# Two attentions with V stationary in column halves and the z of the first SSD group as filler, and an expert scatter kept for the last six pairs

## The chip, the cores and the metric

One core of a Trainium2 chip runs the whole program. The metric is the device time of one execution in microseconds (us). Matrix products run on TensorE (PE; its weight loads are PEld), elementwise work on VectorE (DVE), ScalarE (ACT) and GpSimd (POOL), and SyncE (SP), ACT and POOL issue DMAs. Each engine works through its own queue in order.

## The reference, cut to what matters

Two transformer blocks on 512 tokens of width 1024. The first has spatial gating, a sliding-window attention, an attention to 256 memory tokens, and a gate z. The second has a top-k attention, a state-space branch (SSD) in four groups with a gate z, and a mixture of 32 experts (MoE), two for each token.

```python
# block 1, both attentions: four heads of 64
out = einsum('bnhgqj,bnjhd->bnqhgd', softmax(logits), vb)
y = concatenate([y_a, y_b, y_c]) * silu(z);  x = x + rms_norm(y @ w_out)
# block 2, attention: 16 heads of 64, 4 key/value heads, keys <= query block
o = einsum('bqhgk,bqkhd->bqhgd', softmax(logits), v_sel)
# SSD: conv + silu on xs, B, C; chunked scan; then
y_ssd = group_rmsnorm(y * silu(z)) * g
merged = sigmoid(gate_a) * (y_attn @ w_a) + sigmoid(gate_b) * (y_ssd @ w_b)
x = x + merged @ w_out
# MoE: for each expert e
act = silu(h @ w_gate[e]) * (h @ w_up[e]) * combine[:, e]
out += act @ w_down[e]
```

## The kernel before

The program runs as a chain of stages: block 1 with its attentions (110 to 206 us of the profile), block 2's projections and index scores, block 2's attention (393 to 541), the SSD groups one after another (from 541), the branch merge, and the experts (from about 1010 us to the end). Large products with float32 precision are made of three float32r matmuls of 512 columns each (`gemm_t`, L224 to L226), with the weight split in a high and a low part by ACT (L173) and DVE or POOL (L175). Generators are woven by `mix`: a main generator says how many us of filler it needs at each step, and a filler generator of dense gemms is advanced by so much. Outside the experts, the order within an engine is then made by the compiler's scheduler; in the experts the order on PE is the order of the code.

**Attention of block 1.** `pipeline` runs eight units (two kinds, four query blocks) through five stages `logits`, `expo`, `ptrans`, `pvmul`, `otrans`. `pvmul` takes the transposed probabilities pT (128 keys x 128 queries) as the stationary operand and V (128 x 64) as the moving one (L755), multiplies the result by the reciprocal row sums on DVE (L758), and `otrans` transposes it back by two PE transposes (L768) and a DVE copy (L769). The filler is one u gemm and three z gemms.

**Attention of block 2.** The same five stages for 32 units (four kv heads, two pairs of heads, four query blocks): `pvmul` L1085, the DVE product L1088, the transpose L1098 into a PSUM tile that is held for four units, and an ACT copy L1101. Its filler is `gates`, 16 gemms of 24 matmuls each, the first of which are already used up under the index scores.

**SSD.** `ssd_gemm(g)` makes B and C, xs in two gemms, and z in two gemms; `conv_silu` works on each gemm's output on DVE (L1184, L1190, L1196) and ACT; `silu_from` (L450, L455) works on z. `ssd_chain(g)` is mixed with the gemms of group g + 1. For group 0 all five gemms run ahead of its chain.

**Experts.** There are 16 pairs of experts. For a pair, `gate_up` (L1765, 32 matmul instructions in pairs of column halves) and `down` (L1786, 16 instructions) read weight tiles of 512 KB, twelve for a pair, that SP prefetches in the order of `units`; a new fetch is issued when a tile is read (L1884). Results of most pairs go to a DRAM table by `y_store`, whose DMA is issued on ACT (L1800), and come back by eight indirect DMAs on POOL in `y_fetch` (L1808) and DVE additions (L1810), all at pairs 13 and 14. The pairs in `self.direct` (3, 6, 9, 12, 13, 14, 15) are instead scattered to token rows by matmuls with a one-hot matrix: `slots_t` builds it (L1715, L1720), `y_split` splits the result, `scatter` runs two matmuls (L1871) and a DVE addition (L1873) for each of eight output tiles, in one go after the pair's `down`. Pairs 14 and 15 are scattered in `finish` (L1832 to L1847), which also stores the output. The loop at `for p in range(17)` runs `down(p - 1)` after `gate_up(p)`.

Of the kernel before, what the change touches and what calls it, by code (L numbers as in the profile page):

```python
# [43 lines left out]
class Ker:  # L44
# [412 lines left out]

    def pipeline(self, units, stages, need):
# [65 lines left out]
    def block1(self):  # L524
# [218 lines left out]
        def pvmul(u):  # L743
            kind, n = u
            wk, r, pT = st[u][1], *st[u][4:6]
            po = self.paux()
            nj = wk // P
            for h in range(4):
                for j in range(nj):
                    if kind == 0:  # L750
                        kt = n + 1 - nj + j
                        v = sv[:, kt * P + (h // 2) * 64:kt * P + (h // 2) * 64 + 64]
                    else:
                        v = mv[:, j * 256 + h * 64:j * 256 + h * 64 + 64]
                    nc.tensor.matmul(po[:, h * 64:h * 64 + 64], pT[j][:, h * P:(h + 1) * P], v,  # L755
                                     start=(j == 0), stop=(j == nj - 1))
            o = self.ms([P, 256], "ot")
            nc.vector.tensor_tensor(o.rearrange("p (h d) -> p h d", h=4),  # L758
                                    po[:, :256].rearrange("p (h d) -> p h d", h=4),
                                    r.unsqueeze(2).to_broadcast([P, 4, 64]), op=ALU.mult)  # L760
            st[u] = o

        def otrans(u):
            kind, n = u
            o = st.pop(u)
            po = self.paux()
            for c in range(2):
                nc.tensor.transpose(po[:, c * P:(c + 1) * P], o[:, c * P:(c + 1) * P], self.ident)  # L768
            nc.vector.tensor_copy(c2(oc if kind else ob)[:, :, n * P:(n + 1) * P],  # L769
                                  po[:, :256].rearrange("p (c t) -> p c t", c=2))  # L770
# [21 lines left out]
        mix(self.pipeline(units, (logits, expo, ptrans, pvmul, otrans), 4.5), f2)  # L792
# [77 lines left out]
    def block2(self, hh, hl, ssq):  # L870
# [33 lines left out]
        self.gd = tc.dram_tile([16, P, T], F32, name="scr_g")  # L904

        def gate(i):

            def f(ps):
                t_ = self.t2()
                nc.vector.tensor_tensor(t_, ps[0], rbh, op=ALU.mult)  # L910
                nc.scalar.activation(t_, t_, AF.Tanh)
# [140 lines left out]
        def expo(u):  # L1052
# [6 lines left out]
            r = self.sm([P, 2], "xr")  # L1059
            nc.vector.reciprocal(r, s)  # L1060
            st[u].append(r)
# [17 lines left out]
        def pvmul(u):  # L1079
            kv, c, b = u  # L1080
            po = self.paux()
            r, pts = st[u][2:4]
            for j in range(2):
                for t, pT, i in pts:
                    nc.tensor.matmul(po[:, j * 64:j * 64 + 64], pT[:, i * 256 + j * P:i * 256 + (j + 1) * P],  # L1085
                                     v4[:, t, kv * 64:kv * 64 + 64], start=(t == 0), stop=(t == b))
            o = self.ms([P, P], "ot")
            nc.vector.tensor_tensor(o.rearrange("p (h d) -> p h d", h=2),  # L1088
                                    po[:, :P].rearrange("p (h d) -> p h d", h=2),
                                    r.unsqueeze(2).to_broadcast([P, 2, 64]), op=ALU.mult)  # L1090
            st[u] = o

        def otrans(u):
# [4 lines left out]
            nc.tensor.transpose(po[:, b * P:(b + 1) * P], st.pop(u), self.ident)  # L1098
            if b == NT - 1:
                o = self.t2()  # L1100
                nc.scalar.copy(o, po)  # L1101
# [10 lines left out]
        def attn():  # L1112
            for i, _ in enumerate(self.pipeline(units, (logits, expo, ptrans, pvmul, otrans), 0)):
# [84 lines left out]
    def ssd_gemm(self, g, hh, hl, rb, rbh):  # L1198

        nc = self.nc  # L1200
        u2 = lambda i: [("w2", 2 * (8 + 5 * g + i)), ("w2", 2 * (8 + 5 * g + i) + 1)]
# [21 lines left out]
        return ([self.gemm_t(u2(0), hh, hl, KK, bc_done)] + [self.gemm_t(u2(1 + i), hh, hl, KK, xs_done(i)) for i in range(2)]  # L1223
# [568 lines left out]
    def y_store(self, p, py):  # L1792
# [7 lines left out]
        nc.scalar.dma_start(self.y1d[n:n + P], y)  # L1800

    def y_fetch(self, t):

        nc = self.nc
        x = self.acc[:, t]
        for j in range(2):
            y = self.yf[t % 2 * 2 + j]
            nc.gpsimd.indirect_dma_start(out=y, out_offset=None, in_=self.y1d, in_offset=bass.IndirectOffsetOnAxis(  # L1808
                ap=self.row1[:, t, j:j + 1], axis=0), bounds_check=18 * 64 - 1, oob_is_err=False)
            nc.vector.scalar_tensor_tensor(x, y, self.has1[:, t, j:j + 1], x, op0=ALU.mult, op1=ALU.add)  # L1810
# [12 lines left out]
    def finish(self):  # L1823
# [15 lines left out]
        def late(q, t):  # L1839
# [7 lines left out]
            nc.sync.dma_start(self.out[t][:, s], a)  # L1847
# [39 lines left out]
    def moe_start(self):  # L1887

        self.units = []
        for p in range(17):  # L1890
            self.units += [(e, j) for j in range(4) for e in (2 * p, 2 * p + 1) if p < 16]
            self.units += [(e, j) for j in (4, 5) for e in (2 * p - 2, 2 * p - 1) if p]
# [46 lines left out]
    def moe_body(self, oh, xe):  # L1939
# [5 lines left out]
        at, py = {}, {}  # L1945
# [322 lines left out]
```

## Time and profile before

| | us |
|---|---|
| median of 3 runs (lowest to highest) | 1304.72 (1301.74 to 1309.18) |
| the profiled execution | 1306.37 |
| its span in the trace | 1304.7 |

| engine | busy us of the span |
|---|---|
| PE | 1245.5 |
| PEld | 975.2 |
| DVE | 882.0 |
| ACT | 509.1 |
| POOL | 429.5 |

HBM traffic is 206.0 MB read and 16.1 MB written. Busy time of PE is a union of overlapping, pipelined matmuls, so that what a matmul costs is read from the distance of starts. Ln is line n of the kernel's file.

### The profile page before, as it was taken

The page shows a single profiled execution, that of the slowest core. Times are in us where ns is not written, and L with a number is a line of the kernel's source. Part 1 is how long each engine was busy: PE and PEld are TensorE (multiplying, and loading weights), DVE is VectorE, ACT ScalarE, POOL GpSimd, SP SyncE. Part 2 cuts the span into 40 slices and gives each one's busy share as a digit, 9 for nine tenths or more (in the row PEclk, how much of TensorE's full clock was granted, in tenths as well). Part 3 has the DMA queues.
Part 4 walks back from the last instruction along what each step waited for, and adds up shares of the span by engine and source line. Part 5 has one row for each costly group of instructions (what it writes and reads, how often), then busy time and mean ns, then how long its engine had stood idle before and what let it go on. Part 6 is the DMA issues. An engine that isn't in the chain of part 4 may idle for free. (4 is left out here: it accounts for less than half of the span.)

```text
span 1304.7 us, 18947 instructions
## 1 busy us (share of the span) xinstructions
PE 1245.5 (95%) x7045; PEld 975.2 (75%) x7045; DVE 882.0 (68%) x1700; ACT 509.1 (39%) x942; POOL 429.5 (33%) x474
## 2 busy tenths in 40 slices
PE   6899999999999999999999999999999999999787
PEld 5879888999987888888787887877889744544333
DVE  6598756658998676777988887888683532332255
ACT  6435553355543555443454442443333211111011
POOL 0373323169335431123463343436325110001020
PEclk8899999999999999999999999999999999999889
DMA  7234242052233221134334234385330999999992
GB/s 290 65 92 152 65 144 83 35 160 82 72 106 110 94 98 65 41 116 125 109 96 132 88 105 130 100 288 174 129 135 11 386 374 403 416 414 416 362 412 109
DMA packets 86911, 221.35 MB, mean 170 GB/s; under 512 B 8267, under 2 KB 31467, under 8 KB 86816
## 3 DMA queue, kind: packets, MB, share of 16 engines
q1 hardware_dynamic: 79808, 203.08, 44.6%
q10 hardware_dynamic: 4560, 10.26, 2.1%
q0 software_dynamic: 2448, 6.77, 1.4%
q8 instruction: 56, 0.92, 0.3%
q14 instruction: 39, 0.32, 0.1%
HBM read 205.97 MB, written 16.06 MB: 170 GB/s over the span
## 5 line engine op out<-in xcount | busy, mean ns | idle before, releaser
L175 POOL TENSOR_TENSOR wlo<-tb,whi 128x1024 fp32r<-128x1024 f32 x75 | 191.9, 2559 | 267.7 <-ACT whi L173 267.5
L224 PE MATMUL pmm<-tb,whi 128*128 128x512 f32 x600 | 238.7, 398 | 0.0
L226 PE MATMUL pmm<-tb,wlo 128*128 128x512 f32 x600 | 237.2, 396 | 0.0
L225 PE MATMUL pmm<-tb,whi 128*128 128x512 f32 x600 | 237.0, 395 | 0.0
L173 ACT CAST whi<-tb 128x1024 fp32r<-128x1024 f32 x139 | 144.8, 1044 | 138.6 <-PE pmm L225 57.0
L225 PEld LDWEIGHTS pmm<-tb,whi 128*128 128x128 f32 x600 | 114.0, 190 | 23.6 <-issue 0.9
L226 PEld LDWEIGHTS pmm<-tb,wlo 128*128 128x128 f32 x600 | 113.7, 189 | 24.0 <-issue 0.5
L224 PEld LDWEIGHTS pmm<-tb,whi 128*128 128x128 f32 x600 | 113.8, 190 | 23.2 <-issue 1.2
L175 DVE TENSOR_TENSOR wlo<-tb,whi 128x1024 fp32r<-128x1024 f32 x64 | 82.1, 1284 | 23.2 <-ACT whi L173 23.0
L225 PE MATMUL pmm<-t,whi 128*128 128x512 f32 (+1 forms) x208 | 79.4, 385 | 0.7 <-DVE t L356 0.7
L226 PE MATMUL pmm<-t,wlo 128*128 128x512 f32 (+1 forms) x208 | 79.4, 385 | 0.0
L224 PE MATMUL pmm<-t,whi 128*128 128x512 f32 (+1 forms) x208 | 79.4, 389 | 0.0
L1765 PE MATMUL pmm<-wr,xe 128*64 128x512 f32 x240 | 66.4, 596 | 0.0
L1772 DVE SCALAR_TENSOR_TENSOR th<-th,pmm 128x256 f32<-128x256 f32 x16 | 6.7, 420 | 86.0 <-ACT th L1771 86.0
L1771 ACT ACTIVATE th<-pmm,wcol 128x256 f32<-128x256 f32 x16 | 7.6, 474 | 136.9 <-PE pmm L1765 99.9
L1269 DVE TENSOR_SCALAR t<-t,acs 128x128 f32<-128x128 f32 x128 | 43.8, 408 | 24.2 <-DMA t<-scr_a 24.2
L1190 DVE SCALAR_TENSOR_TENSOR t<-cv,cwh,t 128x512 f32<-128x512 f32 x72 | 56.6, 840 | 0.3 <-ACT t L1187 0.3
L334 PE MATMUL pmm<-whi,tb 128*128 128x256 f32 x192 | 54.8, 285 | 0.0
L336 PE MATMUL pmm<-whi,tb 128*128 128x256 f32 x192 | 54.6, 284 | 0.0
L335 PE MATMUL pmm<-wlo,tb 128*128 128x256 f32 x192 | 54.4, 283 | 0.0
L1057 ACT ACTIVATE tL<-tL,xm 128x128 f32<-128x128 f32 (+3 forms) x64 | 35.4, 554 | 30.6 <-DVE xm L1049 30.4
L225 PEld LDWEIGHTS pmm<-t,whi 128*128 128x128 f32 x208 | 39.2, 188 | 8.4 <-DVE t L356 1.1
(452 smaller groups left out, 2960.3 us busy)
## 6 DMA issues: line engine op xcount, KB each, us to landing
wr<-in_we_dram SPq DMA_DIRECT2D x89, 512.0 KB, 10.1
tb<-in_w_dram SPq DMA_DIRECT2D x78, 512.0 KB, 3.6
tb<-in_we_dram SPq DMA_DIRECT2D x53, 512.0 KB, 10.1
rx<-in_we_dram SPq DMA_DIRECT2D x50, 512.0 KB, 9.0
tb<-in_wo_dram SPq DMA_DIRECT2D x16, 512.0 KB, 3.7
tb<-in_wg_dram SPq DMA_DIRECT2D x16, 512.0 KB, 3.6
t<-scr_a SPq DMA_DIRECT2D x16, 512.0 KB, 5.8
tb<-in_wsb_dram SPq DMA_DIRECT2D x16, 512.0 KB, 3.7
```

The source lines that it names most:

```text
L173: nc.vector.tensor_copy(hi, raw) if dve_hi else nc.scalar.copy(hi, raw)
L175: f = lambda: (nc.gpsimd if pool_lo else nc.vector).tensor_tensor(lo, raw, hi, op=ALU.subtract)
L224: nc.tensor.matmul(ps[c][:, :n], hi[:, s], xh[k], start=first, stop=False)
L225: nc.tensor.matmul(ps[c][:, :n], hi[:, s], xl[k], start=False, stop=False)
L226: nc.tensor.matmul(ps[c][:, :n], lo[:, s], xh[k], start=False, stop=last)
L334: nc.tensor.matmul(o, xh[k][:, ts], hi[:, s], start=(k == 0 and t % 2 == 0), stop=False, **kw)
L335: nc.tensor.matmul(o, xh[k][:, ts], lo[:, s], start=False, stop=False, **kw)
L336: nc.tensor.matmul(o, xl[k][:, ts], hi[:, s], start=False, stop=(k == 7), **kw)
L1057: nc.scalar.activation(L3[:, j], L3[:, j], AF.Exp, bias=m[:, j:j + 1], scale=0.125, accum_out=s[:, j:j + 1])
L1190: nc.vector.scalar_tensor_tensor(y, x[:, i:T + i], w(ct, i), y, op0=ALU.mult, op1=ALU.add)
L1269: nc.vector.tensor_scalar(h8(ab)[:, h], h8(ab)[:, h], self.acs[:, c, 8 * g + h:8 * g + h + 1], 0.0, op0=ALU.subtract, op1=ALU.min)
L1765: nc.tensor.matmul(pg[h * 64:h * 64 + 64], xe[d][:, e + h], w[:, j * 512:(j + 1) * 512], start=(d == 0), stop=(d == 7))
```

## The change

**Attention.** In both `pvmul`, V (64 columns) becomes the stationary operand and pT the moving one (128 columns), two heads side by side in the column halves of PE, so that the result is already transposed. `otrans` is dropped and the pipeline has four stages. The reciprocal sums are spread over the rows by a new helper `rcp_t` (two matmuls with the identity for each two heads), copied by ACT, and applied by one DVE product: in block 1 for each unit, in block 2 once for four units.

**z of group 0.** The four 128-row parts of the first SSD group's z become gates 16 to 19: they are computed as filler of block 2's attention, stored to DRAM without the tanh, and loaded by SP in `ssd_gemm(0)` (`z_load`), which applies the tanh on ACT and the product on DVE. The host packs the weights to match.

**Experts.** `direct` becomes 10 to 15; pairs 0 to 9 go through the table, whose store is issued on POOL. The scatter of pair p - 2 is spread in steps of two tiles between the four `gate_up` steps of pair p. `y_fetch` is split in halves at pairs 11 and 12, and the additions (`y_add`) follow at pair 12 and, spread, in pair 14. `down(14)` moves ahead of `gate_up(15)`, in the fetch order too. The one-hot matrices are built when a scatter pair comes up (14 and 15 together). Output stores alternate between SP and ACT.

```diff
+    def rcp_t(self, out, r):
+        for j in range(2):
+            self.nc.tensor.matmul(out[j * 64:j * 64 + 64], r[:, j:j + 1].to_broadcast([P, 64]), self.ident, ...)
 # block 1 pvmul
-                    nc.tensor.matmul(po[:, h * 64:h * 64 + 64], pT[j][:, h * P:(h + 1) * P], v, ...)
+                        nc.tensor.matmul(po[i * 64:i * 64 + 64, c * P:(c + 1) * P], v, pT[j][:, h * P:(h + 1) * P], ...)
+            for c in range(2):
+                self.rcp_t(pr[:, c * P:(c + 1) * P], r[:, 2 * c:2 * c + 2])
+            nc.scalar.copy(rt, pr[:, :256])
+            nc.vector.tensor_tensor(c2(oc if kind else ob)[:, :, n * P:(n + 1) * P], po..., rt..., op=ALU.mult)
-        mix(self.pipeline(units, (logits, expo, ptrans, pvmul, otrans), 4.5), f2)
+        mix(self.pipeline(units, (logits, expo, ptrans, pvmul), 4.5), f2)
 # block 2
-        gates = chain(*[gate(i) for i in range(16)])
+        gates = chain(*[gate(i) for i in range(20)])
+            for t, pT, i in st.pop(u)[2]:
+                for j in range(2):
+                    nc.tensor.matmul(po[j * 64:j * 64 + 64, b * P:(b + 1) * P], v4[:, t, kv * 64:kv * 64 + 64],
+                                     pT[:, i * 256 + j * P:i * 256 + (j + 1) * P], ...)
             if b == NT - 1:
+                for t in range(NT):
+                    self.rcp_t(pr[:, t * P:(t + 1) * P], r[:, t])
+                nc.scalar.copy(rt, pr)
+                nc.vector.tensor_tensor(o, po, rt, op=ALU.mult)
 # ssd_gemm
+        if g == 0:
+            return first + [z_load()]
 # experts
-        self.direct = [3, 6, 9, 12, 13, 14, 15]
+        self.direct = [10, 11, 12, 13, 14, 15]
-        nc.scalar.dma_start(self.y1d[n:n + P], y)
+        nc.gpsimd.dma_start(self.y1d[n:n + P], y)
+            self.units += gu(p) + (dn(p - 1) if 0 < p < 15 else []) + (dn(p) if p > 13 else [])
+            sc = self.scatter((p - 2,)) if p - 2 in self.direct else iter(())
+            ya = self.y_add(1) if p == 14 else iter(())
             for j in range(4):
                 self.gate_up(pg, pair(p, j), xe, 2 * i, j)
+                some(sc, 2)
+                some(ya, 1)
-            nc.sync.dma_start(self.out[t][:, s], a)
+            (nc.scalar if t % 2 else nc.sync).dma_start(self.out[t][:, s], a)
```

## Rows read from the trace of the kernel before

**Rows 1.** The page, part 1: busy time of each engine

```profile
PE 1245.5 (95%) x7045; PEld 975.2 (75%) x7045; DVE 882.0 (68%) x1700; ACT 509.1 (39%) x942; POOL 429.5 (33%) x474
```

**Rows 2.** By stretch: length, busy us (count) of each engine, clock, DMA

```profile
110.00:206.00 96.00, 95.56 (x563) 83.17 (x561) 67.12 (x117) 50.52 (x121) 24.17 (x12) 1.00 0.32 105
393.00:500.00 107.00, 104.66 (x622) 91.49 (x621) 77.55 (x240) 52.99 (x126) 44.84 (x70) 0.98 0.30 94
500.00:541.00 41.00, 38.74 (x308) 35.02 (x307) 31.59 (x118) 25.78 (x74) 2.24 (x4) 1.00 0.15 53
541.00:668.00 127.00, 124.77 (x611) 101.17 (x611) 106.74 (x177) 54.00 (x75) 46.46 (x37) 0.99 0.36 107
...
630.00:660.00 30.00, 29.47 (x145) 23.48 (x146) 27.92 (x47) 13.66 (x17) 12.09 (x8) 0.94 0.29 88
...
1040.00:1276.00 236.00, 220.26 (x1045) 97.52 (x1043) 79.31 (x154) 31.81 (x61) 26.57 (x81) 0.96 1.00 399
1276.00:1304.70 28.70, 21.79 (x88) 11.30 (x84) 13.80 (x21) 4.66 (x8) 0.00 (x0) 0.94 0.21 77
```

**Rows 3.** PE's timeline in block 2's attention: start, us, line, operation, count

```profile
449.05 1.45 PE L1085 MATMUL paux<-t,pT 128*128 128x64 f32 x12
450.34 1.04 PE L1072 MATMUL paux<-cst,tL 128*128 128x128 f32 x8
```

**Rows 4.** PE's timeline in the first SSD group

```profile
610.14 0.39 PE L225 MATMUL pmm<-tb,whi 128*128 128x512 f32 x1
610.37 0.39 PE L226 MATMUL pmm<-tb,wlo 128*128 128x512 f32 x1
610.68 1.09 PE L1282 MATMUL pacc<-t,t 128*64 128x128 f32 x16
611.71 1.13 PE L1287 MATMUL paux<-t,bt 128*128 128x512 f32 x2
```

**Rows 5.** Groups by line: count, busy us, mean ns, idle before

```profile
L1085 PE MATMUL paux<-t,pT 128*128 128x64 f32 x320 | 40.6, 272 | 1.8 <-DVE pT L1075 1.4
...
L755 PE MATMUL paux<-t,t 128*128 128x64 f32 x120 | 14.5, 273 | 0.1
```

**Rows 6.** Groups by line on DVE from 541 to 668 us

```profile
L450 DVE TENSOR_TENSOR mm<-pmm,tb 128x512 f32<-128x512 f32 x6 | 4.0, 681 | 1.9 <-PE pmm L226 1.9
```

**Rows 7.** DMA from 1020 to 1305 us, 40 slices; two issues

```profile
GB/s 411 409 411 408 419 418 309 324 367 408 416 416 420 409 416 418 419 406 417 418 409 418 420 416 410 417 416 412 249 372 387 413 410 419 409 354 1 0 106 193
...
scr_y<-y ACTq DMA_DIRECT2D x9, 512.0 KB, 7.0
...
yf<-scr_y,row POOLq DMA_INDIRECT x8, 8.9
```

**Rows 8.** The timeline of all engines at pair 11 of the experts

```profile
1213.79 0.33 ACTq L1800 DMA_DIRECT2D scr_y<-y  x1
1214.15 1.07 ACT L1754 COPY xe<-paux 128x512 f32<-128x512 f32 x2 [11.50 <-DMA wr<-in_we_dram]
...
1214.79 1.22 PE L1871 MATMUL paux<-y,ohT 128*128 128x512 f32 x2 [8.35 <-ACT xe L1754]
```

**Rows 9.** The timeline of PE and DVE at the end of the experts

```profile
1243.23 5.79 PE L1765 MATMUL pmm<-wr,xe 128*64 128x512 f32 x25
...
1262.50 1.22 PE L1871 MATMUL pacc<-y,ohT 128*128 128x512 f32 x2 [4.16 <-DVE acc L1873]
...
1268.08 5.30 PE L1765 MATMUL pmm<-rx,xe 128*64 128x512 f32 x17
...
1276.23 3.60 PE L1786 MATMUL pmm<-wr,ac 128*64 128x512 f32 x16
...
1279.95 1.17 PE L1871 MATMUL paux<-y,ohT 128*128 128x512 f32 x4
...
1287.81 0.64 PE L1786 MATMUL pmm<-wr,ac 128*64 128x512 f32 x1
...
1298.05 0.69 DVE L1846 TENSOR_TENSOR acc<-pmm,acc 128x512 f32<-128x512 f32 x1 [0.21 <-PE pmm L1832]
```

More of the change, by code (lines that the diff above doesn't have):

```diff
@@ L1080, in pvmul @@
             kv, c, b = u
[L1081 to L1093, printed above, removed]
-            kv, c, b = u
             if b == 0:
@@ L1112, in attn @@
         def attn():
-            for i, _ in enumerate(self.pipeline(units, (logits, expo, ptrans, pvmul, otrans), 0)):
+            for i, _ in enumerate(self.pipeline(units, (logits, expo, ptrans, pvmul), 0)):
                 if i % 8 in (1, 2, 3, 4, 5, 6):
@@ L1200, in ssd_gemm @@
         nc = self.nc
-        u2 = lambda i: [("w2", 2 * (8 + 5 * g + i)), ("w2", 2 * (8 + 5 * g + i) + 1)]
+        u2 = lambda i: [("w2", 2 * (8 + max(5 * g - 2, 0) + i) + j) for j in range(2)]
         d = self.grp[g] = {}
@@ L1799, in y_store, with y_fetch, y_add @@
         n = sum(q not in self.direct for q in range(p)) * P
-        nc.scalar.dma_start(self.y1d[n:n + P], y)
[L1802 to L1810, printed above, removed]
+        nc.gpsimd.dma_start(self.y1d[n:n + P], y)
+    def y_fetch(self, h):
+        for t in (2 * h, 2 * h + 1):
+            for j in range(2):
+                self.nc.gpsimd.indirect_dma_start(
+                    out=self.yf[t % 2 * 2 + j], out_offset=None, in_=self.y1d,
+                    in_offset=bass.IndirectOffsetOnAxis(ap=self.row1[:, t, j:j + 1], axis=0), bounds_check=20 * 64 - 1, oob_is_err=False)
+    def y_add(self, h):
+        for t in (2 * h, 2 * h + 1):
+            x = self.acc[:, t]
+            for j in range(2):
+                self.nc.vector.scalar_tensor_tensor(x, self.yf[t % 2 * 2 + j], self.has1[:, t, j:j + 1], x, op0=ALU.mult, op1=ALU.add)
+                yield 1
     def y_split(self, p, py):
@@ L1994, in moe_body @@
                 elif i == 1:
+                    if p == 1:
+                        pre = self.prep(1)
+                        oh = next(pre)
                     run(pre)
@@ L2000, in moe_body @@
                     some(gg, 4)
-            if p > 1 and p - 2 in self.direct:
-                run(self.scatter((p - 2,)))
-            if p < 15 and p + 1 in self.direct:
-                self.slots_t(p + 1)
-            if p == 12:
+            for k in slots.get(p, ()):
+                self.slots_t(k)
+            if p == 11:
                 self.yf = [self.pg.tile([P, 1024], F32, tag="xe", name=self.nm("yf"), bufs=self.nxe) for _ in range(4)]
@@ L2008, in moe_body @@
                     nc.gpsimd.memset(y, 0.0)
-            if p in (13, 14):
-                for t in range(2):
-                    self.y_fetch(2 * (p - 13) + t)
+                self.y_fetch(0)
+            elif p == 12:
+                run(self.y_add(0))
+                self.y_fetch(1)
+            elif p == 14:
+                down(14, ac)
+        ac = next(at)
+        fin = self.finish()
+        next(fin)
+        down(15, ac)
+        run(fin)
     def moe_more(self):
```

139 lines of the change are left out of this document (74 added, 65 removed).

## The prediction

> **What bounds the kernel now.** The page's first part comes first: PE is busy for 1245.5 of 1304.7 us [rows 1]. That is a union of overlapping matmuls, so the view by stretch is read next, and the distance of starts in PE's timeline behind it. From 110 to 206 us (block 1's attention) PE is busy for 95.6 of 96 us, and from 393 to 500 (block 2's) for 104.7 of 107 [rows 2]: PE work taken out there is time taken out. From 500 to 541, where the gates have run out, PE still works 38.7 of 41 us [rows 2]. From 541 to 668 (SSD group 0 and its chain) PE has 124.8 and DVE 106.7 of 127 us; at 630 to 660 DVE has 27.9 of 30 [rows 2]. There two engines are near their bound. The experts are another kind of stage: 1040 to 1276 runs at 399 GB/s [rows 2], the slices stand at 405 to 420 GB/s but for two dips, and stop at about 1276 [rows 7]. There the weight stream sets the time, until it ends; what then follows, 28.7 us [rows 2], is what PE still has to do.
>
> **Block 1's attention.** Twelve pvmul instructions of the old form lie from 449.05 to 450.34 us, 0.107 each [rows 3]. The new form, 64 stationary columns against 128 moving ones into alternating column halves, is what the SSD chain already runs: 16 instructions from 610.68 to 611.71, 0.064 each [rows 4]. The 120 instructions [rows 5] thus lose 120 x 0.043 = 5.2 us. The 16 transposes of otrans go, at 0.107 (an estimate, from the other 128-column loads [rows 3]) 1.7 us. rcp_t adds 8 units x 4 matmuls of two instructions, 64 x 0.064 = 4.1 us, by the same row, since its form is the same. Net -2.8 us, all on PE's path. ACT gets eight copies, and it has 50.5 of 96 us [rows 2]; DVE gets fewer operations. The step that goes from the pipeline is latency under filler.
>
> **Block 2's attention.** 320 instructions [rows 5] x 0.043 = 13.8 us less; 32 transposes x 0.107 = 3.4 less; 8 x 16 rcp_t instructions x 0.064 = 8.2 more: -9.0. DVE swaps 32 small products for 8 large ones. Four more gates fill most of the stretch in which PE now idles for 41 - 38.7 = 2.3 us [rows 2]; I take -1.5, between 0 and -2.3.
>
> **The moved z.** Group 0's z is 96 matmuls of 512 columns before (2 gemms x 48) and after (4 gates x 24). At 0.23 (610.14 to 610.37 [rows 4]) that is 21.8 us of PE, added to 393-541 and taken from 541-668. PE's sum is zero, so the question is whether the second stretch can shrink by 21.8. Its PE would need 105.2 of the 127 - 21.8 us. DVE loses only four products at 0.68 [rows 6] and two of the four low-part subtractions, some 5 us, and keeps 101. DVE worked at most at 0.93 there (27.9 of 30 [rows 2]), which makes 109 us, 4 more than the full shrink. And the filler that stood between the xs gemms and the chain is gone, so the conv of xs comes late for the chain's transposes, on which PE can wait if it doesn't take the next group's gemms first. Ends: 0 (all hidden) and +21.8 (the stretch doesn't shrink). I take +7, near DVE's row. The stores of the gates (four more issues on ACT's queue, ahead of its copies and casts there) and the four loads on SP's queue, ahead of later weight loads, are 256 KB each in stretches with DMA shares of 0.15 to 0.36 [rows 2]: nothing, unless SP is behind with its weights.
>
> **Experts, the stream.** A pair reads 12 x 0.524 = 6.29 MB, at 417 GB/s [rows 7] 15.1 us. The first dip (309, 324, 367) stays; the second (249, 372, 387) costs (168 + 45 + 30) / 417 x 7.1 = 4.2 us [rows 7]. It has a cause that the change removes: at pair 11 ACT's issue of the table store ran only at 1213.79, ACT's next copy had waited for 11.5 us behind it, and PE for 8.35 on that copy, in the scatter of pair 9 [rows 8]. The store now goes through POOL, and pair 9 isn't scattered. On POOL the queued operations behind a store are the one-hot casts, prep's small copies and the fetches; none is due within one pair. -4.2. More bytes: one more store [rows 7], and a ninth more fetched rows, 0.52 + 0.26 MB (by the code), 1.9 us. The last weights then land 2.3 us earlier, at about 1273.2 instead of 1275.5 in the old frame.
>
> The Trainium skill (Trainium Kernel Development and Optimization, Key Constraints) says that DMAs issued from SP, ACT and POOL run on the same engines and that spreading the issue saves only the issue time. By that rule the moved store is worth nine times 0.33 us of an ACT that has time to spare, so nothing, and the dip would stay; the sum would be 4.2 us higher.
>
> **Experts, the end.** down(15) now begins at 1287.8 [rows 9], 12.3 us behind the stream. In PE's way lie the scatter of pair 12, which stood for 4.16 us on DVE while DVE added fetched rows, then gate_up(15) partly at 1.2 GHz (17 instructions in 5.3 us against 25 in 5.8; the granted clock of 1040 to 1276 is 0.96 [rows 2]), down(14), and the scatter of pair 13 from 1279.95 [rows 9]. After the change a pair at 2.4 GHz needs gate_up 32 x 0.217 = 6.9, down 3.5 [rows 9], a scatter of 16 x 0.23 = 3.7 [rows 4] and about 0.9 for transposes and one-hot: 15.0 us, as long as its weights take. So PE can stay level with the stream, and both fetches and half of the additions lie before pair 13. Behind the landing of gate_up(15)'s weights 5 us of down(15)'s are still to come; they cover act(15) and the early matmuls of finish. down(15) then starts at about 1274 + 1 for late additions = 1275; from there 16.9 us to the end as now (1287.8 to 1304.7): 1291.8, or -13. down(14) hid act(15) before; if that cover fails it costs some 2 us. Ends: -17 (down(15) at the stream's last tile) and -2.3 (PE's lag stays).
>
> **Sum.** -2.8 - 9.0 - 1.5 + 7 - 13 = -19.3 against the span of 1304.7. The profiled execution took 1306.37 with it, 1.6 above the median of 1304.72, so the median should fall to 1285.4.
>
> **Rivals.** A: the stretch after 541 doesn't shrink, DVE and the late conv hold it at 127 us. For it: DVE's 0.93; against it: DVE has 5 us less to do, and the next group's gemms can run ahead. +21.8 in place of +7: 1300.2. B: PE's lag at the end stays. For it: PE's 15.0 against 15.1 us for a pair leaves no slack, and DVE waits in order for the fetched rows (y_add at pair 12 stands a pair behind fetches that take 8.9 us to land [rows 7] and wait for the store of pair 9 themselves), with the scatter's additions behind it. -2.3 in place of -13: 1296.1. C, slower: the column halves don't overlap in pvmul and rcp_t, whose stationary operands are other than the chain's. Each of the 440 + 192 instructions then costs 0.107 as now, and the attentions cost 192 x 0.107 - 48 x 0.107 = +15.4 instead of -11.8: 1312.6. All gain is gone when the instruction costs 0.095. Against it: the chain's row has the same shapes and the same alternation [rows 4]. D: the SSD stretch shrinks fully and PE keeps the stream's pace to the last tile: 1274 to 1278.
>
> **How the numbers follow.** The forecast (1279 to 1292) has 0.55, A 0.12, B 0.18, C 0.05, D 0.10. The range goes from 1272 (all good ends: -2.8 - 9.0 - 2.3 - 17 = -31) to 1300 (A or B). A run of this kernel can tell 0.5%, 6.5 us. Faster by more (below 1298.2): the forecast, D, most of B and some of A, 0.82. Within: 0.11. Slower: C and mishaps of A and B together, 0.07.
>
> **What would show it.** Starts of pvmul instructions 0.064 apart, and none at 0.107 (C). The stretch from the end of block 2's attention to the end of group 0's chain at about 112 us, with DVE above 0.9 of it. Block 2's attention longer by some 11 us. No ACT wait of 10 us at a table store, and no second dip. down(15) within 3 us of the last tile's landing, and a granted clock of 1.00 in the last pairs. The prediction is wrong if the first SSD stretch stays at 127 us, or if the expert stream shows a new dip at pairs 12 to 14, where POOL and DVE wait for fetched rows.

## The result, and the profile after

| | before | after |
|---|---|---|
| median, us | 1306.61 (20 runs, 1301.74 to 1314.71) | 1316.94 (20 runs, 1311.30 to 1321.40) |
| profiled execution | 1306.37 | 1311.84 |
| its span | 1304.7 | 1310.2 |

The ratio is 1.0062, 95% interval 1.0047 to 1.0078: slower by some 8 us, where 19 us less were forecast. The profiled execution of after lies near its lowest time; sizes in us are taken from the ratio, places from the trace.

The view by stretch of after (length; busy us and count of PE, PEld, DVE, ACT, POOL; granted clock; DMA share; GB/s):

```profile
394.20:500.00 105.80, 103.49 (x660) 81.45 (x660) 78.11 (x229) 54.68 (x131) 41.26 (x62) 0.98 0.29 93
500.00:561.00 61.00, 59.55 (x463) 47.10 (x463) 35.31 (x110) 29.27 (x74) 9.90 (x15) 1.00 0.28 90
561.00:686.00 125.00, 114.11 (x564) 90.92 (x561) 109.92 (x180) 54.97 (x78) 41.59 (x37) 0.97 0.39 110
605.00:630.00 25.00, 22.85 (x127) 16.89 (x126) 24.96 (x31) 14.14 (x23) 10.29 (x8) 1.00 0.45 119
630.00:660.00 30.00, 26.70 (x150) 20.79 (x149) 30.00 (x55) 12.46 (x16) 10.70 (x9) 1.00 0.43 114
660.00:686.00 26.00, 20.57 (x89) 17.00 (x88) 21.80 (x28) 11.43 (x17) 11.83 (x10) 0.87 0.26 82
1042.30:1279.00 236.70, 226.50 (x1040) 93.83 (x1040) 75.57 (x148) 32.95 (x62) 31.97 (x90) 0.99 1.02 409
1279.00:1310.20 31.20, 22.83 (x93) 11.46 (x91) 11.30 (x18) 3.40 (x6) 0.00 (x0) 0.93 0.20 73
```

The last two rows run from the experts' first gate_up to the end of the weight stream (by the slices of the DMA view), and from there to the end of the span. The same two of before:

```profile
1036.30:1275.50 239.20, 223.47 (x1060) 98.69 (x1061) 79.74 (x155) 31.81 (x61) 26.57 (x81) 0.96 1.01 399
1275.50:1304.70 29.20, 22.29 (x92) 11.45 (x88) 13.80 (x21) 4.66 (x8) 0.00 (x0) 0.94 0.21 79
```

Against [rows 2]: block 2's attention is 19 us longer, where some 11 were forecast (21.8 of z less 9.0 and 1.5). The stretch behind it now has DVE busy for all of 605 to 660, and PE, which had worked 0.98 of it, works 0.91. In the experts the weight stream ends 2.5 us earlier after the first gate_up (236.7 us, 239.2 before), but what follows it is 2.0 us longer (31.2, 29.2): the stage as a whole lasts 267.9 us and lasted 268.4.

Six rows of PE's timeline in block 2's attention of after (start, us, line, operation, count) show what the attention's sum lacked:

```profile
448.01 0.61 PE L461 MATMUL paux<-cst,xr 128*64 128x128 f32 x8
448.55 0.44 PE L1076 MATMUL paux<-cst,tL 128*128 128x128 f32 x2
448.74 0.48 PE L224 MATMUL pmm<-tb,whi 128*128 128x512 f32 x1
449.05 0.40 PE L225 MATMUL pmm<-tb,whi 128*128 128x512 f32 x1
449.38 0.66 PE L1091 MATMUL pacc<-pT,t 128*64 128x128 f32 x8
449.97 0.44 PE L1049 MATMUL paux<-t,t 128*128 128x384 f32 x1
```

Between two gemm instructions the starts are 0.23 apart in the median, as in [rows 4] (the one at 448.74 stands behind transposes, and its record is 0.48 us long, not 0.40). From the gemm instruction at 449.05 to the first pvmul at 449.38 it is 0.33. Eight pvmul instructions take 0.59 with the step to the logits behind them, not 8 x 0.057.

PE's waits in the first SSD stretch of after (line waited for; us in total, times, longest), the two largest:

```profile
PE paux L369 <- DVE t L393: 5.4, 1, 5.4
PE paux L1264 <- DVE t L1307: 1.5, 1, 1.5
```

The 5.4 us stand at the end of group 0's chain: PE has used up the gemms of group 1 and waits for DVE's sum of squares.

In the experts, one slice line of the DMA view of after (1020 to 1310 us, 40 slices):

```profile
GB/s 359 414 409 407 409 421 418 384 325 400 409 413 420 419 411 414 420 411 414 419 419 411 414 418 414 415 416 412 404 414 416 405 409 418 414 298 0 0 87 208
```

The first dip stays, the second [rows 7] is gone. And PE's timeline in pair 13 of after:

```profile
1237.78 1.94 PE L1778 MATMUL pmm<-tb,xe 128*64 128x512 f32 x8
1239.65 0.73 PE L1890 MATMUL paux<-y,ohT 128*128 128x512 f32 x2
1245.84 1.22 PE L1890 MATMUL pacc<-y,ohT 128*128 128x512 f32 x2 [5.46 <-DVE acc L1892]
1246.99 3.68 PE L1778 MATMUL pmm<-rx,xe 128*64 128x512 f32 x8
```

DVE's timeline in the same pair:

```profile
1238.63 2.60 DVE L1828 SCALAR_TENSOR_TENSOR acc<-yf,has,acc 128x1024 f32<-128x1024 f32 x2
1241.26 1.29 DVE L1892 TENSOR_TENSOR acc<-paux,acc 128x512 f32<-128x512 f32 x2
1242.46 2.60 DVE L1828 SCALAR_TENSOR_TENSOR acc<-yf,has,acc 128x1024 f32<-128x1024 f32 x2
1245.10 0.69 DVE L1892 TENSOR_TENSOR acc<-pacc,acc 128x512 f32<-128x512 f32 x1
```

PE stood 5.46 us for the scatter's addition, which stood behind four additions of fetched rows; the trace has a granted clock of one half (1.2 GHz) from 1244.3, late in that wait, to 1251.1, and eight gate_up instructions take 3.68 us where they take 1.94 at 1237.78.

### The profile page after: what moved, and what is told of

It is laid out like the page before. It is cut to its first block, busy times and chain, and to the rows that moved or that the text cites. A ratio compares the mean times of both kernels' runs of the same rounds, so it can differ in the third digit from the quotient of the medians.

```text
span 1310.2 us, 19184 instructions
## 1 busy us (share of the span) xinstructions
PE 1247.1 (95%) x7172; PEld 946.6 (72%) x7172; DVE 868.5 (66%) x1658; ACT 511.9 (39%) x949; POOL 428.8 (33%) x484
## 5 line engine op out<-in xcount | busy, mean ns | idle before, releaser
L175 POOL TENSOR_TENSOR wlo<-tb,whi 128x1024 fp32r<-128x1024 f32 x75 | 189.2, 2523 | 319.9 <-ACT whi L173 304.6
L1778 PE MATMUL pmm<-wr,xe 128*64 128x512 f32 x256 | 74.0, 599 | 1.8 <-DMA wr<-in_we_dram 1.8
L1189 DVE SCALAR_TENSOR_TENSOR t<-cv,cwh,t 128x512 f32<-128x512 f32 x72 | 65.4, 960 | 0.3 <-ACT t L1186 0.3
L336 PE MATMUL pmm<-whi,tb 128*128 128x256 f32 x192 | 54.5, 284 | 0.0
L1778 PEld LDWEIGHTS pmm<-wr,xe 128*64 128x64 f32 x256 | 20.6, 136 | 38.7 <-issue 30.0
## 6 DMA issues: line engine op xcount, KB each, us to landing
wr<-in_we_dram SPq DMA_DIRECT2D x89, 512.0 KB, 10.3
tb<-in_we_dram SPq DMA_DIRECT2D x53, 512.0 KB, 10.7
```

What stands on the lines that cost most here:

```text
L175: f = lambda: (nc.gpsimd if pool_lo else nc.vector).tensor_tensor(lo, raw, hi, op=ALU.subtract)
L336: nc.tensor.matmul(o, xl[k][:, ts], hi[:, s], start=False, stop=(k == 7), **kw)
L1189: nc.vector.scalar_tensor_tensor(y, x[:, i:T + i], w(ct, i), y, op0=ALU.mult, op1=ALU.add)
L1778: nc.tensor.matmul(pg[h * 64:h * 64 + 64], xe[d][:, e + h], w[:, j * 512:(j + 1) * 512], start=(d == 0), stop=(d == 7))
```

## The experiments: which part lost the time

Three kernels make one part of the change alone, on the kernel before. Their medians and ratios are against runs of before on the same chip.

**e1_att**, the attentions alone.

```diff
+    def rcp_t(self, out, r): ...
 # both pvmul: V stationary in halves; otrans dropped
 # z, gates and experts as before
```

> The kernel before with the V-stationary halves in both attentions alone (z of the first SSD group stays in its group, experts as before). Theory 1 (the halves pay, and what the whole change lost was lost by the moved z): block 1 gives about 1.1 us and block 2's attention about 9 us less PE time, so 8 to 11 us faster than before, near 1297; the first SSD stretch stays at its 127 us. Rival (the attention with four stages has less slack and waits more, so PE's saving turns into gaps): within 3 us of before.

Measured: 1306.79 against 1307.66, ratio 0.9998 (0.9977 to 1.0018). Not 8 to 11 us faster: nothing. The rival's figure came true; how much of its mechanism did is counted at e5. The stretch of block 2's attention, from its first logits to its last, is 142.1 us long (393.0 to 535.1), before 141.2 (393.3 to 534.5).

**e2_z**, the moved z alone.

```diff
-        gates = chain(*[gate(i) for i in range(16)])
+        gates = chain(*[gate(i) for i in range(20)])
+        if g == 0:
+            return first + [z_load()]
```

> The kernel before with the z of the first SSD group moved into the gates alone. Theory 1 (DVE sets the first SSD stretch, so PE's time that is added ahead of it is not given back): block 2's attention stage 22 to 27 us longer, the stretch behind it 9 to 14 us shorter, so 10 to 15 us slower than before, near 1318. Rival (the loss came from the two parts together: the halves use up the slack in which the gates would lie): within 4 us of before.

Measured: 1316.83 against 1307.66, ratio 1.0071 (1.0055 to 1.0088), 9.3 us slower: just under theory 1's 10 to 15. The attention's stretch grew by 19.7 us, the one behind it shrank by 11.8 (rows below).

**e3_moe**, the expert part alone.

```diff
-        self.direct = [3, 6, 9, 12, 13, 14, 15]
+        self.direct = [10, 11, 12, 13, 14, 15]
 # y_store on POOL, scatter between the gate_up steps, y_fetch in halves, y_add, down(14) ahead
```

> The kernel before with the expert part alone. Theory 1 (the second dip of the stream goes, 4 to 5 us, but PE stays as far behind the stream's end as before, since the scatter between the gate_up steps makes a pair dearer for PE and the additions of fetched rows hold DVE): within 3 us of before. Rival (the expert part gains what was predicted, and only the later start or the changed fetch order of the whole change hid it): 10 to 13 us faster, near 1294.

Measured: 1308.82 against 1307.66, ratio 1.0010 (0.9990 to 1.0029). Theory 1. The three parts make -0.3 + 9.3 + 1.3 = +10.3 us, the whole change +8.1 (6.1 to 10.2): they add within their intervals of some 2.5 us each, and no interplay larger than that is seen.

**e4_store**, only the store's queue.

```diff
-        nc.scalar.dma_start(self.y1d[n:n + P], y)
+        nc.gpsimd.dma_start(self.y1d[n:n + P], y)
```

> The kernel before with one word changed: the store of a pair's result is issued on GpSimd's queue, not on ScalarE's. Theory 1 (the issue that ScalarE held behind caused the second dip): no wait of 10 us on ScalarE behind a store and no dip of the stream between pairs 11 and 12; 2 to 4 us faster, and the rest of it hidden by TensorE's lag at the end. Rival (the dip came from the scatter of pair 9, which still runs here, or from the fetches): the dip stays and the time is within 1 us of before.

Measured: 1304.03 against 1307.66, ratio 0.9974 (0.9955 to 0.9994), 3.4 us faster. ACT's wait of 11.5 us [rows 8] is gone, and so is the dip. DMA of this kernel from 1150 to 1260 us, 40 slices:

```profile
GB/s 414 420 423 417 420 420 410 407 410 416 420 422 420 413 414 408 408 408 414 423 419 422 417 417 407 410 416 408 422 419 422 404 405 405 407 410 417 417 422 414
```

The scatter of pair 9 still runs here, so the cause was the queue, as the prediction had it. The prediction weighed against this the Trainium skill's word (Trainium Kernel Development and Optimization, Key Constraints) that spreading the issue saves only the issue time; by that nothing was to be had, and 3.4 us were: what the moved issue freed was ACT's queue, with the copies that PE waited for.

## The experiments: the attention

**e5_group** keeps e1's products of the second attention back until four query blocks are ready.

```diff
             kv, c, b = u
-            if b == 0:
-                st["o"] = self.pacc()
-            po = st["o"]
-            for t, pT, i in st.pop(u)[2]:
-                for j in range(2): ...
             if b == NT - 1:
+                po = self.pacc()
+                for q in range(NT):
+                    for t, pT, i in st.pop((kv, c, q))[2]:
+                        for j in range(2): ...
```

> The first experiment's kernel (V-stationary halves in both attentions, nothing else) with the second attention's products kept back and run once for four query blocks, 40 of them and the 8 of the sums in a row; five more buffers for the transposed probabilities. The same instructions, but PE changes between full-width and column-half work some 8 times there instead of some 40. Theory 1 (each change costs about 0.1 us on the way in and 0.1 on the way out, as the starts in the trace of the first experiment show: 0.32 from a gemm to a pvmul against 0.23 inside the gemm, 0.20 from a pvmul to a transpose against 0.06 inside): some 30 pairs of changes at 0.2 are 6 us less, near 0.995 of before. Rival (the lost gain is waiting in a pipeline of four stages): longer bursts wait more, within 2 us of before or slower.

Measured: 1299.87 against 1306.55, ratio 0.9952 (0.9932 to 0.9971). The stretch of the attention in e1, by the view of stretches:

```profile
393.00:535.10 142.10, 135.91 (x954) 106.39 (x953) 104.56 (x323) 75.56 (x191) 45.95 (x74) 0.99 0.27 84
```

and in e5:

```profile
393.70:529.10 135.40, 130.56 (x955) 107.27 (x953) 106.39 (x324) 74.53 (x191) 46.20 (x74) 0.99 0.28 88
```

Same instructions, 6.7 us less. Counted in PE's timeline from the first logits to the last product, with the idle time taken out of the distances of starts:

```
                                  before    e1     e5
column-half instructions               0   448    448
changes into column halves             0    41     25
changes out of them                    0    41     25
median start to start, us:  gemm -> gemm 0.227, gemm -> transpose 0.231, gemm -> pvmul 0.318
                            pvmul -> transpose: before 0.112, in halves 0.203
                            gemm -> pvmul: before 0.232
                            mean inside a run of pvmul: before 0.107, in halves 0.057
first logits to last product, us   148.5   149.1  142.4
of it PE idle, us                    4.9     6.9    5.6
```

A change costs 0.318 - 0.231 = 0.09 us on the way in and 0.203 - 0.057 = 0.15 on the way out, 0.23 for the pair; 41 pairs are 9.6 us. A part of that stood in the prediction's 0.064 already, since its row of 16 instructions ends with a step out. Against its sum the 448 instructions cost 448 x 0.057 + 9.6 - 448 x 0.064 = 6.4 us more, of the 9.0 that it had found. With PE's idle time taken out, e1 needs 142.2 us where before needs 143.6, 1.4 less, and its idle time is 2.1 us longer, as e1's rival had it. So the changes are the larger part of the lost gain, and not all of it. 16 pairs fewer are 3.7 of the 6.7 us that e5 gained, and 1.3 are idle time, to which the five more buffers may have helped; the rest is not separated. With idle time taken out, e5 needs 136.8 us, 6.8 less than before. The scheduler still cuts the runs, 25 of them and not 8. The Trainium skill names such a cost without a figure (TensorEngine Tiling (Array Packing), Key Properties: changing the tiling mode drains the engine); the rows agree and give it one.

## The experiments: the experts

**e6_adds** spreads the additions of fetched rows in e3.

```diff
-            ya = self.y_add(1) if p == 14 else iter(())
+            ya = self.y_add(p // 2 - 6) if p in (13, 15) else iter(())
-            elif p == 12:
-                run(self.y_add(0))
+            elif p == 13:
                 self.y_fetch(1)
```

> The third experiment's kernel (expert part alone) with the first half of the additions of fetched rows spread over the gate_up steps of pair 13, the second fetch behind them and its additions over pair 15. Theory 1 (four additions of 1.28 us in one go hold the scatter's additions on DVE, PE waited 5.5 us on them, and then ran 6.8 us at half clock, 3.4 lost): PE's wait in pair 13 goes, the granted clock stays at 1.0 there, and the time falls by 5 to 9 us against the third experiment, to 0.994 to 0.997 of before. Rival (PE's lag is its own work, and a wait less is only a wait elsewhere): within 2 us of the third experiment, 1.001 of before.

Measured: 1304.43 against 1306.55, ratio 0.9967 (0.9944 to 0.9989); e3 had 1.0010. Theory 1, at its lower end. The 60 us from 1215 us of e3, by the view of stretches:

```profile
1215.00:1275.00 60.00, 54.49 (x214) 19.73 (x212) 34.89 (x49) 6.34 (x12) 10.58 (x11) 0.94 1.03 412
```

and the same of e6:

```profile
1215.00:1275.00 60.00, 59.95 (x254) 22.96 (x254) 34.60 (x51) 8.68 (x16) 10.10 (x11) 1.00 1.03 412
```

PE goes from 54.5 to 59.95 busy us, the clock from 0.94 to 1.00, with the same DVE work. From the first gate_up to the end, the expert stage lasts 259.0 us in the trace of e6 and 268.4 in that of e3; the two spans differ by less, 6.6 us, since this execution of e6 begins the experts 2.8 us later (1044.4, 1041.6).

**e7_block** runs e3's scatter in one go.

```diff
                 self.gate_up(pg, pair(p, j), xe, 2 * i, j)
-                some(sc, 2)
```

> The third experiment's kernel with each pair's scatter run in one go behind its four gate_up steps, not two tiles after each. Theory 1 (each change between gate_up's column halves and the scatter's full width costs 0.2 us in and out; three fewer for each of four pairs): PE needs some 2.5 us less, and the time falls by 1 to 3 us against the third experiment. Rival (the spread is what lets DVE's additions keep up with PE, eight products need eight PSUM tiles and there are fewer): PE waits on DVE in every scatter, and the time rises by 2 to 6 us.

Measured: 1320.06 against 1306.55, ratio 1.0088 (1.0056 to 1.0121), some 10 us above e3: theory 1 missed, and the rival's 2 to 6 were too few. PE's largest waits from 1190 us on:

```profile
PE pacc L1877 <- DVE acc L1879: 13.8, 3, 6.9
```

PE stands for DVE's additions in three pairs, and the granted clock is one half for two stretches of 10.2 us (from 1249.3 and 1276.6).

**e10_both** puts e5's attentions and e6's experts together.

```diff
+ e5_group's pvmul
+ e6_adds' y_add and y_fetch
```

> The attentions of the fifth experiment (halves, second attention's products grouped) with the experts of the sixth (the change's expert part with the additions spread), z of the first group left where it was. If the parts add: 0.9952 and 0.9967 make 0.992 of before, some 10 us faster. Rival (an expert stage that starts earlier only waits longer for its weight stream, or TensorE's clock takes the gain back): 0.995 or above.

Measured: 1294.18 against 1308.42, ratio 0.9887 (0.9854 to 0.9919), the fastest kernel of the study beside e12. The ratios of e5 and e6 multiply to 0.9919, the upper end of this interval: the parts add, if not more. The 75 us from 1195 us of e10, by the view of stretches:

```profile
1195.00:1270.00 75.00, 74.78 (x323) 30.03 (x319) 41.27 (x60) 11.00 (x20) 12.67 (x14) 1.00 1.03 412
```

The end of its PE timeline, and the slices of its DMA view (1020 to 1295 us):

```profile
1274.49 0.44 PE L1775 MATMUL pacc<-cst,th 128*128 128x128 f32 x2 [1.64 <-DVE th L1771]
1274.69 1.62 PE L1836 MATMUL paux<-y,ohT 128*128 128x512 f32 x6
...
1277.56 0.64 PE L1784 MATMUL pmm<-wr,ac 128*64 128x512 f32 x1
```

```profile
GB/s 411 411 408 408 420 418 405 349 366 400 418 414 419 419 409 415 419 412 414 419 419 410 412 420 411 417 418 415 401 411 416 417 406 411 419 409 229 0 143 167
```

PE is busy throughout at the full clock, and down(15) starts at 1277.56, 16.9 us before the end of the span (1294.5), as before [rows 9]. The stream ends in the slice of 229 GB/s, at about 1267.5 + 6.9 x 229 / 415 = 1271.3, so down(15) is 6.3 us behind it, before 12.3. Without a wait for DVE the gate_ups of pairs 11 to 14 still start 16.4 to 16.5 us apart (1190.9, 1207.4, 1223.8, 1240.2), where a pair's weights take 15.1: here PE's own work sets the pace. The expert stage lasts 259.8 us, 8.6 less than before.

**e11_four** scatters in two runs of four tiles.

```diff
-                some(sc, 2)
+                some(sc, 4 * (j % 2))
```

> The tenth experiment's kernel with the scatter in two runs of four tiles for each pair, not four of two. Theory 1 (a change of PE between halves and full width costs 0.2 us in and out): two pairs of changes fewer for each of four pairs, 1 to 2 us less PE, at most that in time. Rival (DVE must keep up with the tiles of a run, as in the seventh experiment): PE waits for DVE's additions, 1 to 6 us slower.

Measured: 1300.98 against 1308.42, ratio 0.9951 (0.9927 to 0.9975), 7 to 8 us above e10: theory 1 missed again. PE waits 4.0 us on DVE's additions at the next pair's one-hot matrix. In the experts the fewer changes are worth less than the room that DVE gets.

**e12_order** puts down(14) behind gate_up(15) again.

```diff
-            if p < 15:
-                down(p - 1, ac)
-                ac = next(at)
+            down(p - 1, ac)
+            ac = next(at)
```

> The tenth experiment's kernel with the down products of pair 14 behind the gate_up of pair 15 again, in the fetch order too, as in the kernel before. Theory 1 (with down(14) ahead, nothing covers pair 15's activation, PE waits 1.6 us and runs the early products without cover): 1 to 3 us faster than the tenth experiment. Rival (the last weights are then those of two down steps, and more PE work lies behind the stream's end): 1 to 3 us slower.

Measured: 1294.75, ratio 0.9904 (0.9872 to 0.9937): within the interval of e10, which tells neither side from the other.

## The experiments: the moved z

The two stretches, from the first logits to the last and from there to the second group's first chain step, before:

```profile
393.30:534.50 141.20, 137.17 (x875) 120.77 (x873) 105.29 (x347) 75.14 (x191) 46.24 (x73) 0.99 0.26 85
534.50:678.20 143.70, 139.66 (x710) 114.13 (x709) 117.77 (x199) 62.35 (x93) 52.03 (x40) 0.99 0.35 105
```

and in e2:

```profile
400.60:561.50 160.90, 156.77 (x971) 137.31 (x969) 110.86 (x353) 79.66 (x195) 50.99 (x75) 1.00 0.29 94
561.50:693.40 131.90, 120.83 (x614) 97.28 (x613) 115.92 (x193) 57.74 (x89) 40.91 (x38) 0.97 0.38 108
```

They are 292.8 us together, before 284.9. So 7.9 are lost in this execution, 9.3 in the times. In the second stretch PE is idle for 11.1 us where it was for 4.0, and DVE is busy for 0.88 of it where it was for 0.82.

**e8_zpool** gives e2's low parts in that stretch to GpSimd.

```diff
+        self.lo_dve = 0
         f = chain(*self.ssd_gemm(0, hh, hl, rb, rbh))
...
+            self.lo_dve = 2
```

> The second experiment's kernel (the moved z alone) with all low parts of the weights made on GpSimd while groups 0 and 1 are computed; DVE loses some eight operations of 1.22 us in that stretch, GpSimd gains as many of 2.5. Theory 1 (DVE is what keeps the stretch behind block 2's attention from shrinking): 5 to 10 us faster than the second experiment, near 1.000 of before. Rival (the chain's latency, or PE, holds it): within 2 us of the second experiment.

Measured: 1323.5 against 1306.55, ratio 1.0129 (1.0097 to 1.0162), 7 to 8 us slower than e2. Groups by line in the stretch (busy us, mean ns; idle before), three of e2:

```profile
L1197 DVE SCALAR_TENSOR_TENSOR t<-t,t 128x512 f32<-128x512 f32 x12 | 8.2, 684 | 0.3
...
L393 DVE TENSOR_TENSOR t<-t,t 128x512 f32<-128x512 f32 x3 | 2.1, 691 | 0.2
...
L175 POOL TENSOR_TENSOR wlo<-tb,whi 128x1024 fp32r<-128x1024 f32 x8 | 21.2, 2655 | 23.1 <-ACT whi L173 23.1
```

and the same three of e8:

```profile
L1197 DVE SCALAR_TENSOR_TENSOR t<-t,t 128x512 f32<-128x512 f32 x12 | 17.1, 1454 | 1.0 <-ACT t L1194 1.0
...
L393 DVE TENSOR_TENSOR t<-t,t 128x512 f32<-128x512 f32 x3 | 6.7, 2240 | 1.8 <-ACT t L392 1.6
...
L175 POOL TENSOR_TENSOR wlo<-tb,whi 128x1024 fp32r<-128x1024 f32 x15 | 38.3, 2554 | 22.1 <-ACT whi L173 21.0 <-DVE cv L1185 1.1
```

These operations of DVE, with two SBUF operands, have two and three times their length of e2 while GpSimd had more to do (the convolution's, L1191, fell from 1.04 to 0.89). The traces show what stretches them: of the 24 L1197 operations in all of e8, the 11 that no GpSimd operation but a memset overlaps last 0.67 to 0.69 us, the 13 others 1.88 in the mean and up to 2.88. The kernel before has the same split (L1196: 11 at 0.67 to 0.69, 13 with a mean of 1.83), and its twelve in this stretch have a mean of 1.32. So the lengthening is not new in e8; in e2 none of the twelve happened to be stretched. DVE lost seven low parts (8.5 us), and its busy time from the attention's end to the second group's chain didn't fall: 117.4 us, in e2 115.9. So this run says nothing against DVE as the bound: it did not relieve DVE, which it was made to do. The Trainium skill warns of it (Perfetto Trace Analysis, Optimizing Scalar/DVE Operations: the two share an SBUF read port, so moving work between them might not help), and the rows agree.

**e9_zact** gives 32 operations of e2's first chain to ScalarE.

```diff
# for group 0
-                nc.vector.tensor_scalar(h8(ab)[:, h], h8(ab)[:, h], a, 0.0, op0=ALU.subtract, op1=ALU.min)
+                nc.scalar.activation(h8(ab)[:, h], h8(ab)[:, h], AF.Relu, scale=-1.0, bias=a)
...
-            nc.scalar.activation(ab, ab, AF.Exp)
+            nc.scalar.activation(ab, ab, AF.Exp, scale=-1.0)
```

> The second experiment's kernel (the moved z alone) with 32 of DVE's operations in the first group's chain (subtract and cap, 0.485 us each, 15.5 us in all) made by ScalarE instead; GpSimd has no more to do than before. Theory 1 (DVE's work holds the stretch behind block 2's attention; moving it to GpSimd failed because DVE's own operations then waited for GpSimd's): the stretch shrinks by 6 to 12 us against the second experiment, the time is 0.998 to 1.002 of before. Rival (the chain's latency holds it, and ScalarE's operations are in the same chain): within 3 us of the second experiment, 1.007.

Measured: 1315.9 against 1308.42, ratio 1.0057 (1.0034 to 1.0080); e2 had 1.0071. The rival's figure: 1.8 us, not to be told from nothing. DVE's busy time in the stretch fell by 8 us (115.9 to 107.9), the stretch from 131.9 to 130.3, and PE still waits 5.0 us for DVE at the end of the chain (3.1 in e2).

**e13_taps_z** and its control **e14_taps** leave DVE work out.

```diff
-            for i in range(3):
+            for i in range(1 if ct in self.few else 3):
```

> The second experiment's kernel (the moved z alone) with two of the three VectorE taps of the convolution left out for the SSD groups 0 and 1: 24 operations of DVE, 18 to 24 us with their waiting, all in the stretch behind block 2's attention; nothing is given to another engine. Its control is the kernel before with the same left out. Theory 1 (DVE's work keeps the stretch from shrinking): the stretch gives back nearly all of the 21.8 us, and the time is within 3 us of the control. Rival (the latency of the chain without z as cover): it stays 6 to 10 us above the control, with PE waiting at the end of group 0's chain.

> The kernel before with two of the three VectorE taps of the convolution left out for the SSD groups 0 and 1, as the control for the thirteenth experiment. PE is the bound of that stretch here (124.8 of 127 us busy), so both theories expect within 4 us of before.

Measured: leaving the taps out changes the routing further on, so that the program runs its part for overfull experts (11378 and 11375 us), and the total times can't be set against before; e14's expectation on the time missed for that reason. The two stretches lie ahead of it. Those of e13:

```profile
395.20:556.40 161.20, 157.79 (x970) 138.57 (x970) 110.94 (x352) 79.75 (x194) 51.09 (x75) 0.99 0.30 94
556.40:677.80 121.40, 114.78 (x593) 93.02 (x592) 93.56 (x167) 56.77 (x89) 40.49 (x38) 0.97 0.39 112
```

and of e14:

```profile
392.60:533.80 141.20, 137.16 (x875) 120.79 (x873) 105.36 (x347) 75.13 (x191) 46.26 (x73) 0.99 0.27 85
533.80:673.40 139.60, 135.94 (x689) 111.52 (x688) 97.02 (x174) 61.88 (x94) 45.26 (x40) 0.98 0.36 105
```

With less work on DVE the second stretch gives back 139.6 - 121.4 = 18.2 us of the 20.0 that the first one grew, where it gave back 11.8 of 19.7 with all of it. The loss falls from 7.9 to 1.8. That is theory 1; the rival's 6 to 10 did not come. But the taps that are left out lie on the chain's way through the convolution too, so that this pair of runs doesn't tell DVE's load from the time that its operations take on that way.

**e15_half** moves only half of z.

```diff
-        gates = chain(*[gate(i) for i in range(20)])
+        gates = chain(*[gate(i) for i in range(18)])
-            return first + [z_load()]
+            return first + [z_load(), self.gemm_t(u2(3), hh, hl, KK, z_done(1))]
```

> The second experiment's kernel with only half of the z of group 0 moved into the gates (two gates, 10.9 us of PE); the other z product stays behind the xs products. Theory 1 (DVE's work sets the shortest length of the stretch): the first part that is moved is given back, up to the slack of DVE, and the loss is under a third of the full one, within 3 us of before. Rival (each moved product takes its cover with it, in proportion): half the loss, 4 to 6 us slower, 1.003 to 1.0045.

Measured: 1308.29 against 1306.78, ratio 1.0007 (0.9988 to 1.0027). Half the move loses 0.9 us, the whole 9.3: not in proportion. Its two stretches:

```profile
392.80:542.60 149.80, 146.44 (x922) 129.64 (x921) 108.32 (x348) 77.43 (x192) 48.64 (x74) 0.99 0.28 90
542.60:679.60 137.00, 131.04 (x662) 106.08 (x661) 112.56 (x195) 60.27 (x91) 49.63 (x39) 0.98 0.37 108
```

The second one gives back 143.7 - 137.0 = 6.7 us of the 8.6 that the first one grew; the whole move gave back 11.8 of 19.7, so 5.1 of the further 11.1. The first half comes back for the most part, the second by less than half, as theory 1 has it.

## Why the prediction was wrong

**Block 1's attention: -2.8 forecast, -1.2 in the traces** of after and e1 (from its first logits to the first gemm of the stage behind it, 108.4 us, 109.6 before). The sign held.

**Block 2's attention: -10.5 forecast, nothing came** in the time of e1. The step that failed is the price of an instruction. 0.064 [rows 4] is right for a run of 16 with its step out (0.057 inside a run), and rival C, at 0.107 for each, did not come. What the sum left out is the change between full-width and column-half work. It stood in the same rows: [rows 4] have 0.31 from the last gemm instruction to the first of the chain's (610.37 to 610.68) where 0.23 lies between two gemm instructions. The chain pays it once for 16 instructions; the attention pays it 41 times for 448, by the table at e5 6.4 us above the sum. The stalls, -1.5 forecast: in after, which has the four more gates, PE's idle time from the first logits to the last product is 3.8 us where it was 4.9; in e1, which lacks them, 6.9.

**The moved z: +7 forecast, +9.3 measured** (e2), inside the ends that were given. DVE was named as the engine that holds the stretch, and e13, e14 and e15 bear that out for most of the loss. Two terms were mis-sized. Between the same points DVE's work fell by 1.9 us (117.8 to 115.9), not by 5, and DVE filled 0.88 of the stretch, not 0.93: 115.9 us at 0.93 would be 124.6, and the stretch took 131.9. (The forecast's figures are for 541 to 668, which ends 10 us before the second group's chain begins.) Why DVE doesn't fill it is open: PE's wait at the end of the chain (5.4 us in after, and a clock of 0.87 in 660 to 686) points to the time that DVE's operations take one after another, and so does e9, which took 8 us off DVE within the chain and gained 1.8, not to be told from nothing; e13 leaves 1.8 us of loss, but it shortens that time too.

**Experts, the stream: -4.2 for the dip, measured -3.4** (e4). Right in mechanism and size; with the added bytes the stream ends 2.5 us earlier, 2.3 forecast.

**Experts, the end: -10.7 forecast (the -13 without the stream's -2.3), nothing came.** The failing step is that PE can stay level with the stream. Two terms were off. The interleaved gate_up and scatter take four steps of 3.0 us (1.87 from 1237.78 to 1239.65 in the rows of pair 13, and 1.15 from 1245.84 to 1246.99), 12.0 and not 6.9 + 3.7 = 10.6, so that a pair needs 12.0 + 3.5 + 0.9 = 16.4 us of PE against the stream's 15.1; the pairs of e10, without waits, take as long. And the additions of pair 12 cost a 5.46 us stall and then 3.4 us at the lower clock level; the forecast had them out of the way. Rival B named this place and gave 1296.1. Spreading the additions brings back 5.5 us of the time (e6 against e3), and 9.4 of the expert stage in the traces; in e10 the lag is half of what it was before, and not the 3 us that were forecast. In after, down(15) starts at 1293.26, 14 us behind the stream's end at 1279.0:

```profile
1287.37 1.19 PE L1890 MATMUL paux<-y,ohT 128*128 128x512 f32 x4
1290.20 0.44 PE L1790 MATMUL pacc<-cst,th 128*128 128x128 f32 x2 [1.64 <-DVE th L1786]
1290.39 1.62 PE L1851 MATMUL paux<-y,ohT 128*128 128x512 f32 x6
...
1293.26 0.64 PE L1799 MATMUL pmm<-wr,ac 128*64 128x512 f32 x1
```

The cover that down(14) gave to act(15) is gone, as the prediction had priced it (1.64 us of wait, 2 forecast), but e12, which restores it, is not faster than e10 by more than its interval.

**The sum.** No attention gain (+13.3), 2.3 more for z and +1.3 in place of -13 for the experts are 29.9 above the forecast of 1285.4: 1315.3, from a before of 1304.7. The before of these comparisons lies at 1306.6, the change at 1316.9. The range ended at 1300 because A and B were each set against a full attention gain; B came whole, A in part (the stretch gave back 11.8 of the 19.7 us), and the gain not at all. (Its lower end, -31 from 1304.7, is 1273.6 and not 1272, which changes nothing here.) The rival on the slower side (C) had the right place, the column halves, and the wrong mechanism, so that its 0.05 of chance hung on something that the row of the chain spoke against.

## What to carry to other kernels

A price for one instruction taken from a long run holds only in long runs: count how often the engine changes between full-width and column-half work, look at the distance of starts across one such change, and group the products before judging the form. Work may be moved ahead of a stretch only as far as the second engine of that stretch has slack; here half of it cost 0.9 us and the whole 9.3. A burst of additions on DVE in front of one that PE waits for costs its own length and then again what PE loses at the lower clock; spread in the steps of the stage it left PE no wait here (e6).

## What the runs showed of the hardware

- A change of PE from full-width to column-half matmuls costs 0.09 us, the way back 0.15 (medians of the distance of starts, block 2's attention).
- A DVE operation with two SBUF operands on 128 x 512 (L1197, in before L1196) lasts 0.67 to 0.69 us in before and e8 where no GpSimd operation but a memset overlaps it (11 of 24 in each), and 1.83 and 1.88 in the mean, up to 2.88, where one does. Such time counts as DVE's busy time.
- In after, PE waited 5.46 us up to 1245.84, and the granted clock was one half from 1244.3 to 1251.1 (6.8 us); in before it was one half for 10.2 us twice (from 1209.1 and 1260.3), at PE's waits of 8.35 us [rows 8] and 4.16 us [rows 9]; in e10, where PE has no wait over 0.2 us between 1195 and 1270, it stayed at 1.00.
